# Progress-tied weight transfers, re-laid FFN buffers and epilogues in parts, in an eight-core hybrid decoder step

## The chip, the cores and the metric

The kernel runs on all 8 cores of one Trainium2 chip (two dies of four cores), one prompt sequence and 16 sample tokens per core. The metric is the device time of the slowest core, in microseconds (us). A run is called slow when some of its cores were granted a visibly lower TensorE clock and took longer; such runs are left out of all comparisons. Profiles show one execution. Where I give the idle time of TensorE by stage, I summed "idle before" over the pieces of its order of instructions; a mean is over the eight cores of one profiled execution. The stages are: start (to 125 us), middle (255 to 560 us, the passage from the mixer to the FFN), and tail (from TensorE's last instruction to the end of the span). Between 125 and 255 us and after 560 us little is idle.

## The reference, cut to what matters

```python
h = rmsnorm(x, g_pre_mix)
u, v, bg, cg, ga, gb = split(h @ w_in)                   # 1024 -> 4096
a = multiscale_pool(u, ...)                              # causal windows 2, 4, 8, 16, then w_pool
b = (bg * causal_dwconv(cg * v)) @ w_conv_out
x = x + rmsnorm((sigmoid(ga) * a + sigmoid(gb) * b) @ w_o, g_post_mix)
h = rmsnorm(x, g_pre_ffn)
gate, val = split(causal_dwconv(h @ w_up))               # 1024 -> 2 x 2816
x = x + rmsnorm((silu(gate) * val) @ w_down, g_post_ffn)
```

A core has 2080 tokens. Phase A (the mixer) takes them in five tiles of 416, phase B (the FFN) in six of 344.

## The kernel before

Every operation is put into a list with the buffers that it reads and writes. A small list scheduler then models durations and fixes the order of instructions on each engine: among the operations that are ready it takes the one that was listed first. Waits follow from the buffers' dependencies only. A tile's two epilogues, the small work after its mixing, are the residual (scale, add the reloaded x, square, store) and the normalisation (eight products and the h2T store).

One input projection block, F, has 16 groups of 8 matmuls (128); mixing, Bfull, has 8 merge steps of 21 matmuls and an output projection, WO, of 64. The order is F(0), F(1), Bfull(0), F(2), Bfull(1), F(3), Bfull(2), F(4), Bfull(3), Bfull(4), then phase B. XR is the buffer into which x is read again for the residual; H2S holds the normalised result, which the h2T store takes to memory; WO writes its squares over H2S.

```python
def F(t, hooks={}):
    for i in range(16):
        F_block(t, i, hooks)
    if t < NTA - 1:                      # the last columns become the next tile's first: the halo copies
        S.add("pool", lambda e: e.tensor_copy(out=U.ap[:, :, 1:16], in_=U.ap[:, :, NA + 1:UW]), ...)
        S.add("pool", lambda e: e.tensor_copy(out=P.ap[:, :, 2:4], in_=P.ap[:, :, NA + 2:NA + 4]), ...)
    ...
# start: weights in order, the conversion to bf16 done by POOL's transfers
for i in range(4):
    wload(W_IN, w_in, i, 1, BL)
load_x(1, 2)
for i in range(4, 16, 2):
    wload(W_IN, w_in, i, 2, BL)
...
# passage: FFN weights, as fast as their buffers come free
    if t == NTA - 1:
        for i in range(4):
            wload(W_UP, w_up, 4 * i, 4, BL)
    ...
    Bfull(t, hooks)
    if t + 2 < NTA:
        F(t + 2, {3: [lambda: epi_r(t)]})      # the whole residual epilogue in one place
for i in range(4, 11):
    wload(W_UP, w_up, 4 * i, 4, BL)
for m in range(8):
    wload(W_DN, w_dn, m, 1, FC * 128)
...
# end: residual added in memory by accumulating transfers from POOL
for q in range(4):
    dve(... Y *= rstd ...)
    pool_dma(yT[...], Y.ap[...], ..., acc=True, mx=4096)
```

Of the kernel before, what the change touches and what calls it, by code (L numbers as in the profile page):

```python
# [12 lines left out]
NS = 16  # L13
D = 1024
KC = 8
# [41 lines left out]
class Sched:  # L57
# [10 lines left out]
    def add(self, eng, fn, r=(), w=(), dma=False, dur=0.0, byts=0, pri=0, tab=None):  # L68
# [22 lines left out]
        deps = set(raw)  # L91
        for d in oth:
            dop = self.ops[d]
            if dop.eng == eng and eng == "pe":
                continue
            deps.add(d)
# [132 lines left out]
def build_nc():  # L229
# [77 lines left out]
    X = al(KC, NA)  # L307
    H = [al(KC, NA, True) for _ in range(2)]
    UW = NA + 16
    U = al(4, UW)  # L310
    PW = NA + 8
# [5 lines left out]
    MERGED = al(KC, NA, True)  # L317
# [3 lines left out]
    STG = al(1, 200)  # L321
    R = Buf(SBW - KC * NA, KC, NA, False)
# [5 lines left out]
    ST_POOL = Buf(X.off, 4, 15 * NS, False)  # L328
    ST_CONV = Buf(X.off + 960, 4, 2 * NS, False)

    bl = Alloc(W0 + 32 * 512, SBW)
    W_UP2 = bl(12, KC * 128, True)
    W_UP = Buf(W0, 44, KC * 128, True)
    W_DN = bl(8, FC * 128, True)
    H2W = NB + 8
    H2 = [bl(KC, H2W, True) for _ in range(2)]
    G = [bl(FC, NB, True)]
    NSET = 4
    TB = [bl(2, NB) for _ in range(NSET - 1)]
    TB.append(Buf(SD.off + NA, 2, NB, False))  # L340
    assert TB[-1].off + TB[-1].words <= SD.off + SD.words
    PRE = bl(44, NS)
# [6 lines left out]
    ST_FFN = Buf(H2[1].off, 44, 2 * NS, False)  # L349
    assert ST_FFN.words <= H2[1].words  # L350
    assert NTB % 2 == 0
    TAIL = Buf(H2[0].off, 1, 44 * 18, False)

# [26 lines left out]

    def pe(mms, r, w, n, start=True, stop=True):
        def f(e):
            last = len(mms) - 1
            for i, (o, l, x) in enumerate(mms):
                ins = e.matmul(o, lhsT=l, rhs=x, start=(start and i == 0), stop=(stop and i == last))  # L385
            return ins
        S.add("pe", f, r, w, dur=len(mms) * (n / 2.4 + 2.5))

    def sp_dma(out, in_, r, w, byts, pri=0):
        S.add("sp", lambda e: e.dma_start(out=out, in_=in_), r, w, dma=True, byts=byts, pri=pri)  # L390

    def pool_dma(out, in_, r, w, byts, acc=False, mx=8192, pri=0):
        if acc:
            S.add("pool", lambda e: e.dma_start(out=out, in_=in_, accum_op=ALU.add, max_dma_last_dim=mx),  # L394
                  r, w, dma=True, byts=byts, pri=pri)
        else:
            S.add("pool", lambda e: e.dma_start(out=out, in_=in_, max_dma_last_dim=mx), r, w, dma=True,  # L397
                  byts=byts, pri=pri)
# [3 lines left out]
    def wload(buf, src, lo, n, per, src_lo=None):  # L402
        src_lo = lo if src_lo is None else src_lo
        dst = buf.flat[:, lo * per:(lo + n) * per]
        pool_dma(dst, src[:, src_lo * per:(src_lo + n) * per], [], [buf.t(lo, n)], 128 * n * per * 4)
# [5 lines left out]
    def load_x(t, parts):  # L411
        st = KC // parts
        X = xbuf(t)
        for q in range(parts):
            sp_dma(X.flat[:, q * st * NA:(q + 1) * st * NA], xT[t][:, q * st * NA:(q + 1) * st * NA],
                   [], [X.t(q * st, st)], 128 * st * NA * 4)
# [120 lines left out]
    def F(t, hooks={}):  # L537
        for i in range(16):
            F_block(t, i, hooks)
        if t < NTA - 1:  # L540
            S.add("pool", lambda e: e.tensor_copy(out=U.ap[:, :, 1:16], in_=U.ap[:, :, NA + 1:UW]),
                  [U.t()], [U.t()], dur=250)
            S.add("pool", lambda e: e.tensor_copy(out=P.ap[:, :, 2:4], in_=P.ap[:, :, NA + 2:NA + 4]),  # L543
                  [P.t()], [P.t()], dur=200)
# [65 lines left out]
    def epi_r(t):  # L610
        rstd(XSQ2, 1, NA)
        tt = pool_tt if t == NTA - 1 else dve
        for q in range(2):
            sp_dma(XR.flat, xT[t][:, 4 * q * NA:4 * (q + 1) * NA], [], [XR.t()], 128 * 4 * NA * 4)
            for h in range(2):
                k, n = 4 * q + 2 * h, 2
                r = R.ap[:, k:k + n, :]
                tt(lambda e, r=r: e.tensor_tensor(out=r, in0=r, in1=SD.ap[:, 1, :].unsqueeze(1).to_broadcast([128, 2, NA]),
                                                   op=ALU.mult), [R.t(k, n), SD.t(1, 1)], [R.t(k, n)], n * NA, pri=BG)
                tt(lambda e, r=r, h=h: e.tensor_tensor(out=r, in0=r, in1=XR.ap[:, 2 * h:2 * h + 2, :], op=ALU.add),  # L620
                    [R.t(k, n), XR.t(2 * h, 2)], [R.t(k, n)], n * NA, pri=BG)
                act(lambda e, k=k, r=r: e.activation(out=XSQ2.ap[:, k:k + 2, :], in_=r, func=AF.Square),  # L622
                    [R.t(k, n)], [XSQ2.t(k, n)], n * NA, pri=BG)
            sp_dma(yT[:, 4 * q:4 * q + 4, t * NA:(t + 1) * NA], R.ap[:, 4 * q:4 * q + 4, :],
                   [R.t(4 * q, 4)], [("y", t, q)], 128 * 4 * NA * 4)

    def epi_x1(t):
        rstd(XSQ2, 2, NA)
        for k in range(KC):
            if t == NTA - 1:  # L630
                act(lambda e, k=k: e.activation(out=R.ap[:, k, :], in_=R.ap[:, k, :], func=AF.Copy, scale=cc(C_G3 + k)),
                    [R.t(k, 1), KCST, ("y", t, k // 4)], [R.t(k, 1)], NA, ap=1)
                pool_tt(lambda e, k=k: e.tensor_tensor(out=H2S.ap[:, k, :], in0=R.ap[:, k, :], in1=SD.ap[:, 2, :], op=ALU.mult),  # L633
                        [R.t(k, 1), SD.t(2, 1)], [H2S.t(k, 1)], NA)
                continue
            dve(lambda e, k=k: e.scalar_tensor_tensor(out=H2S.ap[:, k, :], in0=R.ap[:, k, :], scalar=cc(C_G3 + k),  # L636
                                                      in1=SD.ap[:, 2, :], op0=ALU.mult, op1=ALU.mult),
                [R.t(k, 1), SD.t(2, 1), KCST], [H2S.t(k, 1)], NA, stt=True, pri=BG)
        for q in range(2):
            sp_dma(h2T[:, 4 * q:4 * q + 4, t * NA:(t + 1) * NA], H2S.ap[:, 4 * q:4 * q + 4, :], [H2S.t(4 * q, 4)],  # L640
                   [("h2", t, q)], 128 * 4 * NA * 2)
# [13 lines left out]
    def pair(t, j):  # L655
# [5 lines left out]
        for half in range(2):  # L661
            b = next_bank()
            blk = 2 * j + half
            wb = W_UP.ap[:, blk, :].rearrange("p (k c) -> p k c", k=KC)
            pe([(bank(b, NBH), wb[:, k, :], hb.ap[:, k, 0:NBH]) for k in range(KC)], [W_UP.t(blk, 1), hb.t()],
# [35 lines left out]
    def epi_y(t):  # L701
        rstd(YSQ, 0, NB)
        lo = T0B + t * NB
        for q in range(4):
# [7 lines left out]
    def pre_ffn():  # L712
# [5 lines left out]
        S.add("pool", lambda e: e.tensor_tensor(out=PRE.ap, in0=st[:, :, 0, :], in1=w0b, op=ALU.mult),  # L718
              [ST_FFN.t(), KCST], [PRE.t()], dur=du)
        S.add("pool", lambda e: e.tensor_tensor(out=st[:, :, 0, :], in0=st[:, :, 1, :], in1=w1b, op=ALU.mult),  # L720
              [ST_FFN.t(), KCST, PRE.t()], [ST_FFN.t()], dur=du)
        S.add("pool", lambda e: e.tensor_tensor(out=PRE.ap, in0=PRE.ap, in1=st[:, :, 0, :], op=ALU.add),
              [ST_FFN.t(), PRE.t()], [PRE.t()], dur=du)


    load_x(0, 4)
# [6 lines left out]
    for i in range(4):  # L733
        wload(W_IN, w_in, i, 1, BL)
    load_x(1, 2)
    for i in range(4, 16, 2):
        wload(W_IN, w_in, i, 2, BL)
# [4 lines left out]
    load_x(2, 2)  # L742
    wload(W_POOL, w_pool, 0, 8, 128)
    for i in range(8):
        wload(W_IN, w_in, 16 + 2 * i, 2, BL)
        wload(W_CO, w_co, i, 1, 512)
    for i in range(4):
        wload(W_O, w_o, 2 * i, 2, BL)

    def pre_hook(t):  # L750
# [7 lines left out]
        def nh():  # L758
            prenorm_h(t)
            if t == NTA - 1:  # L760
                load_states()
            elif t > 1:
                load_x(t + 1, 2)
# [15 lines left out]
    sp_dma(o_pool_sa, st_pool_d[:, :, NS:15 * NS], [], ["o3"], 128 * 896 * 4)  # L779
    sp_dma(o_conv_st, st_conv_d, [], ["o5"], 128 * 128 * 4)  # L780
    sp_dma(o_ffn_st, st_ffn_d, [], ["o7"], 128 * 1408 * 4)
    F(1)
    for t in range(NTA):
        hooks = {}
        if t + 2 < NTA:
            sq, st, nh = pre_hook(t + 2)
            hooks = {0: [sq], 4: [st], 7: [nh]}
        if t == NTA - 1:
            hooks = {0: [lambda: epi_r(t - 1)], 5: [lambda: epi_x1(t - 1)]}
        if t == NTA - 1:  # L790
            for i in range(4):
                wload(W_UP, w_up, 4 * i, 4, BL)
        if 0 < t < NTA - 1:
            hooks.setdefault(4, []).append(lambda: epi_x1(t - 1))
        Bfull(t, hooks)
        if t + 2 < NTA:
            F(t + 2, {3: [lambda: epi_r(t)]})
    for i in range(4, 11):
        wload(W_UP, w_up, 4 * i, 4, BL)
    for m in range(8):  # L800
        wload(W_DN, w_dn, m, 1, FC * 128)
    load_h2(0)
    pre_ffn()
    WD = {2: 0, 5: 1, 8: 2, 10: 3, 13: 4, 15: 5, 18: 6, 21: 7}
    for t in range(NTB):
        for j in range(FC):
            pair(t, j)
            if t == 0 and j == 3:
                epi_r(NTA - 1)
            if t == 0 and j == 8:  # L810
                load_h2(1)
            if t == 0 and j == 17:
                epi_x1(NTA - 1)
# [143 lines left out]
```

## Time and profile before

| | before |
|---|---|
| time, median of 3 runs | 977.16 us (967.63 to 992.52, the last one slow) |
| span of core 0, the slowest | 978.1 us, of the others 962.5 to 971.5 |
| TensorE busy, core 0 / mean of 8 cores | 854 / 840 us |
| TensorE idle, start / 125 to 255 / middle / after 560 us, mean | 43.1 / 6.2 / 58.0 / 3.9 us |
| tail, mean | 18.1 us |

How to read it: TensorE has 1920 matmuls of 416 columns and 3216 of 344 or 346, at full clock 810 us (the working is in the prediction). What exceeds 810 us of busy time is low clock; cores 0 and 1 had more of it in this execution (granted 0.930, busy 854 and 857 us) than the other six (0.949 to 0.953, 835 us on the mean). The rest of the span is idle time, and each hole has to be read from what ended it.

### The profile page before, as it was taken

What the parts mean: (1) busy time and instruction counts of PE and PEld (TensorE: products, weight loads), DVE (VectorE), ACT (ScalarE), POOL (GpSimd) and SP (SyncE); (2) the same over time, 40 slices, a digit from 0 to 9 for tenths busy, and PEclk for the clock granted to TensorE, in tenths of its full rate; (3) what the DMA queues carried; (4) which work ended last, traced back from release to release, by engine and by line L of the source; (5) the groups of instructions that cost most, each with busy time, mean ns of one, the idle gap of its engine ahead of it and who ended that gap; (6) DMA issues with size and microseconds to landing.
All of it is one profiled execution on the core that took longest, in us unless ns stands there. A gap on an engine that the chain in (4) does not pass through costs nothing.

```text
span 978.1 us, 16306 instructions; the slowest of 8 cores (962.5 to 978.1 us)
## 1 busy us (share of the span) xinstructions
PE 854.3 (87%) x5136; PEld 512.0 (52%) x5136; DVE 536.2 (55%) x959; ACT 457.0 (47%) x880; POOL 221.9 (23%) x288
## 2 busy tenths in 40 slices
PE   1964999899899399964879999999999999999992
PEld 0432555455455144422546666666666666666661
DVE  1533647657667352640457656665666665675611
ACT  3212254545554044431667555654655564555531
POOL 2111000000002000030286322422432332253322
PEclk9977999999999778866789999999999999999996
DMA  9999130340327945889522000500400130040044
GB/s 201 174 186 166 24 105 24 83 140 22 100 79 114 194 127 94 168 191 174 92 71 70 32 1 2 88 1 2 74 16 1 40 49 1 2 59 1 2 75 58
DMA packets 37667, 75.82 MB, mean 78 GB/s; under 512 B 2096, under 2 KB 26544, under 8 KB 37568
## 3 DMA queue, kind: packets, MB, share of 16 engines
q0 software_dynamic: 16160, 37.56, 25.8%
q1 hardware_dynamic: 21424, 37.23, 12.5%
q8 instruction: 43, 0.70, 0.3%
q14 instruction: 40, 0.33, 0.1%
HBM read 82.14 MB, written 22.98 MB: 107 GB/s over the span
## 4 chain that ended last, share of the span: by engine, by line
PE 66%; DMA 16%; DVE 6%; issue 4%; ACT 3%; POOL 2%; POOLq 0%; DVEq 0%; SPq 0%; ACTq 0%
PE ps L385 66%; DMA big<-w_in 8%; DMA big<-xT 5%; DMA h2T<-big 3%; DVE big L673 1%; DVE big L476 1%; DVE big L620 1%; ACT L423 1%; ACT big L669 1%; DVE big L452 1%; POOL big L633 1%; DVE big L583 0%; DVE big L581 0%; DVE big L636 0%; POOL big L677 0%
## 5 line engine op out<-in xcount | busy, mean ns | idle before, releaser
L385 PE MATMUL ps<-big 128*128 128x346 bf16 (+2 forms) x5136 | 854.3, 331 | 105.9 <-ACT big L595 15.3
L385 PEld LDWEIGHTS ps<-big 128*128 128x128 bf16 x5136 | 512.0, 100 | 447.8 <-issue 136.4
L673 DVE SCALAR_TENSOR_TENSOR big<-ps,big 128x344 f32<-128x344 f32 x528 | 282.8, 572 | 186.7 <-ACT big L669 154.5
L686 POOL TENSOR_TENSOR big<-big 128x344 bf16<-128x344 f32 x132 | 120.5, 915 | 263.5 <-DVE big L673 219.5
L669 ACT ACTIVATE big<-ps,big 128x344 f32<-128x344 f32 x264 | 140.6, 545 | 72.9 <-PE ps L385 69.1
L685 ACT ACTIVATE big<-big 128x344 f32<-128x344 f32 x132 | 64.3, 488 | 39.5 <-DVE big L673 36.9
L566 ACT ACTIVATE big<-ps 128x416 f32<-128x416 f32 x80 | 39.6, 517 | 66.9 <-PE ps L385 64.7
L577 DVE SCALAR_TENSOR_TENSOR big<-ps,big 128x416 f32<-128x416 f32 x40 | 26.0, 649 | 51.1 <-PE ps L385 48.0
L696 ACT ACTIVATE big<-ps,big 128x344 f32<-128x344 f32 x48 | 26.0, 547 | 56.8 <-PE ps L385 50.5
L593 ACT ACTIVATE big<-ps,big 128x416 f32<-128x416 f32 x40 | 24.6, 620 | 38.7 <-PE ps L385 38.6
L705 DVE TENSOR_TENSOR big<-big 128x688 f32<-128x688 f32 x24 | 19.4, 870 | 36.3 <-ACT big L425 36.3
L394 POOL DMA_DIRECT2D yT<-big x24 | 29.5, 1880 | 36.8 <-DVE big L705 36.8
L521 DVE TENSOR_TENSOR big<-ps,big 128x416 f32<-128x416 f32 x20 | 11.6, 586 | 47.0 <-ACT big L519 25.2
L622 ACT ACTIVATE big<-big 128x832 bf16<-128x832 f32 x20 | 17.8, 892 | 41.2 <-DVE big L620 40.7
L397 POOL DMA_DIRECT2D big<-w_up x11 | 7.8, 712 | 123.6 <-PE ps L385 123.6
L452 DVE SCALAR_TENSOR_TENSOR big<-big 128x416 f32<-128x416 f32 x40 | 25.9, 650 | 14.0 <-ACT big L449 11.9
L595 ACT ACTIVATE big<-ps 128x416 bf16<-128x416 f32 x40 | 20.1, 530 | 28.9 <-DMA h2T<-big 28.9
L476 DVE TENSOR_TENSOR big<-big 128x430 f32<-128x430 f32 (+3 forms) x50 | 30.0, 601 | 2.7
L543 POOL COPY big<-big 128x8 f32<-128x8 f32 x4 | 1.4, 346 | 131.6 <-DVE big L452 131.6
L435 DVE SCALAR_TENSOR_TENSOR big<-big 128x416 bf16<-128x416 f32 x40 | 23.0, 646 | 12.4 <-ACT big L425 10.8
L620 DVE TENSOR_TENSOR big<-big 128x832 f32<-128x832 f32 x16 | 16.0, 1020 | 25.0 <-DMA big<-xT 25.0
L429 ACT ACTIVATE big<-big 128x832 bf16<-128x832 f32 x20 | 17.1, 887 | 25.9 <-DMA big<-xT 25.9
(49 smaller groups left out, 312.4 us busy)
## 6 DMA issues: line engine op xcount, KB each, us to landing
big<-xT SPq DMA_DIRECT2D x18, 832.0 KB, 7.0
big<-w_up POOLq DMA_DIRECT2D x11, 1024.0 KB, 14.3
yT<-big SPq DMA_DIRECT2D x10, 832.0 KB, 5.3
yT<-big POOLq DMA_DIRECT2D x24, 344.0 KB, 8.3
big<-w_in POOLq DMA_DIRECT2D x14, 512.0 KB, 28.1
big<-w_dn POOLq DMA_DIRECT2D x8, 704.0 KB, 16.9
h2T<-big SPq DMA_DIRECT2D x10, 416.0 KB, 4.0
big<-h2T SPq DMA_DIRECT2D x6, 692.0 KB, 4.9
```

Source lines behind the costliest of these rows:

```text
L385: ins = e.matmul(o, lhsT=l, rhs=x, start=(start and i == 0), stop=(stop and i == last))
L394: S.add("pool", lambda e: e.dma_start(out=out, in_=in_, accum_op=ALU.add, max_dma_last_dim=mx), r, w, dma=True, byts=byts, pri=pri)
L452: dve(lambda e, k=k: e.scalar_tensor_tensor(out=cv, in0=p[:, 2 + k:2 + k + NA], scalar=cc(C_WC + 4 * k + c), in1=cv, op0=ALU.mult, op1=ALU ...
L476: dve(lambda e, nx=nx, cur=cur, s=s, lo2=lo2: e.tensor_tensor(out=nx.ap[:, 0, lo2:UW], in0=cur[:, lo2:UW], in1=cur[:, lo2 - s:UW - s], op= ...
L566: act(lambda e, b=b, g=g: e.activation(out=GT.ap[:, g, :], in_=bank(b, N), func=AF.Sigmoid), [("ps", b)], [GT.t(g, 1)], N, psum=True, tab= ...
L577: dve(lambda e: e.scalar_tensor_tensor(out=A_, in0=bank(bp, N), scalar=cc(C_PS + m), in1=A_, op0=ALU.mult, op1=ALU.mult), [("ps", bp), GT. ...
L620: tt(lambda e, r=r, h=h: e.tensor_tensor(out=r, in0=r, in1=XR.ap[:, 2 * h:2 * h + 2, :], op=ALU.add), [R.t(k, n), XR.t(2 * h, 2)], [R.t(k, ...
L669: act(lambda e, b=b, fj=fj, tt=tt: e.activation(out=tt, in_=bank(b, NB), func=AF.Copy, scale=cc(C_WF + fj)), [("ps", b), KCST], [tok], NB, ...
L673: dve(lambda e, b=b, fj=fj, tt=tt, k=k: e.scalar_tensor_tensor(out=tt, in0=ps[:, b * 512 + k:b * 512 + k + NB], scalar=cc(C_WF + 44 * k + ...
L685: act(lambda e: e.activation(out=g, in_=g, func=AF.Silu), [T.t(0, 1)], [T.t(0, 1)], NB, tab="silu")
L686: S.add("pool", lambda e: e.tensor_tensor(out=gb.ap[:, j, :], in0=g, in1=v, op=ALU.mult), [T.t()], [gb.t(j, 1)], dur=NB * 2.17 + 100)
L696: act(lambda e: e.activation(out=Y.ap[:, m, :], in_=bank(b, NB), func=AF.Copy, scale=cc(C_G4 + m)), [("ps", b), KCST], [Y.t(m, 1)], NB, ps ...
```

## The change

Its intent: let the FFN weights arrive during the last mixing stages, at TensorE's pace rather than in a burst, by laying them over mixer buffers that are dead by then; keep the epilogues from blocking an engine for long; order the first transfers; shorten the end. The core of the diff, with cuts marked:

```diff
-    def add(self, eng, fn, r=(), w=(), ..., tab=None):
+    def add(self, eng, fn, r=(), w=(), ..., tab=None, after=()):
+        deps.update(x.idx for x in after if x is not None)
 ...
+    W_UP = Blocks([W0 + BW * i for i in range(16)] + [U.off + BW * i for i in range(13)] +
+                  [W0 + BW * (16 + i) for i in range(15)])
+    W_DN = Buf(W0 + 31 * BW, 8, FC * 128, True)
 ...
-    def pool_dma(out, in_, r, w, byts, acc=False, mx=8192, pri=0):
+    def pool_dma(out, in_, r, w, byts, acc=False, mx=4096, pri=0, after=()):
 ...
+    def wup(n):          # the next n blocks of W_UP, tied to TensorE's latest listed matmul
+            pool_dma(dst.flat, w_up[:, i * BL:k * BL], [], [dst.t()], ..., after=[last_pe[0]])
 ...
-            S.add("pool", lambda e: e.tensor_copy(out=U.ap[:, :, 1:16], ...
+            act(lambda e: e.activation(out=U.ap[:, :, 1:16], in_=U.ap[:, :, NA + 1:UW], func=AF.Copy), ...
 ...
+    wd = [wload(W_IN, w_in, i, 1, BL, after=[x0[1]]) for i in range(16)]
+    load_x(1, 2, after=[wd[5]])
 ...
     wload(W_POOL, w_pool, 0, 8, 128)
+    for i in range(16):
+        w = wload(W_IN, w_in, 16 + i, 1, BL)
+        if i % 2:
+            wload(W_CO, w_co, i // 2, 1, 512)
 ...
+            for i in range(4):
+                hooks[i] += er[1 + i:2 + i]          # residual epilogue, a quarter per merge step
+            o = 1 if t == NTA - 1 else 0
+            hooks[4 + o] += ex[0:2]                  # normalisation, in three more steps
+            hooks[5 + o] += ex[2:5]
+            hooks[6 + o] += ex[5:9]
 ...
+        if t >= NTA - 2:
+            for m in range(8):
+                if t == NTA - 2 or m % 2:
+                    hooks[m].append(lambda: wup(2))
 ...
+                add = pool_tt if q < 2 else dve      # last tile: residual added on chip
+                add(lambda e, yq=yq, q=q: e.tensor_tensor(out=yq, in0=yq, in1=X1.ap[...], op=ALU.add), ...)
+                sp_dma(yT[:, 2 * q:2 * q + 2, lo:lo + NB], yq, ...)
```

The epilogues' background priority in the scheduler (`pri=BG`) went with the split. Three copies of states inside memory moved to phase B.

## The prediction

> **What bounds the kernel now.** I read the page first, then the windows of busy time, the order of instructions on TensorE, and the chain of work that ended last. All lines are of core 0, the slowest (978.1 us; the other cores 962.5 to 971.5). The page's row of 40 slices (24.5 us each), cut to TensorE, its clock and the DMA engines:
>
> ```profile
> PE   1964999899899399964879999999999999999992
> PEclk9977999999999778866789999999999999999996
> DMA  9999130340327945889522000500400130040044
> ```
>
> TensorE is the bound nearly everywhere, with three holes: the first four slices, the stretch from the 13th to the 21st, and the last slice. Both inner holes lie under a DMA row near 9, and the clock is low in the same places. The windows give sizes (columns: stretch, length, busy us and count for PE, PEld, DVE, ACT, POOL, then clock, DMA share, GB/s):
>
> ```profile
> 206.00:300.00 94.00, 89.44 (x506) 49.32 (x507) 60.04 (x104) 48.94 (x86) 1.92 (x3) 1.00 0.25 76
> 344.00:402.00 58.00, 57.31 (x261) 28.27 (x262) 25.12 (x42) 25.88 (x45) 2.31 (x4) 0.79 0.55 112
> 402.00:440.00 38.00, 28.90 (x127) 13.57 (x125) 19.78 (x31) 11.15 (x17) 8.54 (x9) 0.73 0.89 194
> 440.00:470.00 30.00, 14.70 (x63) 7.21 (x62) 0.00 (x0) 5.06 (x11) 2.15 (x3) 0.67 1.04 173
> 700.00:850.00 150.00, 150.00 (x1026) 100.27 (x1025) 97.45 (x179) 81.87 (x164) 49.14 (x51) 1.00 0.15 25
> ```
>
> A 416-column matmul takes 89.44/506 = 177 ns at full clock, but 57.31/261 = 220 ns from 344 to 402 us, at clock 0.79; a 344-column one takes 146 ns. The floor follows: the kernel has 1920 matmuls of 416 columns (phase A, the mixer, five token tiles) and 3216 of 344 or 346 (phase B, the FFN, six tiles): 1920 x 0.177 + 3216 x 0.146 = 340 + 470 = 810 us. The page has 854 us busy, so a low clock costs 44 us, and 978 - 854 = 124 us are idle.
>
> Where the idle time lies, from TensorE's order of instructions (start, length, then the idle time before and its releaser):
>
> ```profile
> 23.81 23.14 PE L385 MATMUL ps<-big 128*128 128x416 bf16 x120 [7.32 <-DVE big L435]
> 54.05 4.97 PE L385 MATMUL ps<-big 128*128 128x416 bf16 x16 [7.10 <-DMA big<-w_in]
> 61.82 11.54 PE L385 MATMUL ps<-big 128*128 128x416 bf16 x56 [2.80 <-DVE big L435]
> 86.33 3.97 PE L385 MATMUL ps<-big 128*128 128x416 bf16 x11 [12.97 <-ACT big L519]
> ```
>
> 43 us are lost before 86.3 us. The last hole, 13 us, is not a missing weight. ScalarE waits to write the conv buffer until POOL has copied its halo, and POOL is held in its instruction order by weight-transfer issues:
>
> ```profile
> 84.17 1.15 POOL L397 DMA_DIRECT2D big<-w_o  x2 [1.56 <-DMA big<-w_in]
> 85.32 0.20 POOL L543 COPY big<-big 128x8 f32<-128x8 f32 x1
> ...
> 85.67 0.93 ACT L519 ACTIVATE big<-ps 128x416 f32<-128x416 f32 x2 [25.64 <-POOL big L543]
> ```
>
> The second hole: the FFN weights begin at 296 us and are issued as fast as buffers come free, and small transfers that the epilogues need sit among them. The three longest such pieces of the chain of work:
>
> ```profile
> 314.36 27.03 DMA big<-xT
> ...
> 405.27 17.58 DMA big<-xT
> ...
> 439.86 29.34 DMA h2T<-big
> ```
>
> The 832 KB reload of x usually lands in 7 us (median); here it took 27. The h2T store frees the buffer that the last output projection writes, so TensorE stood still for 12 us. From 300 to 540 us the windows sum to 49 us idle. The tail is 18 us: TensorE ends at 960.1, VectorE scales until 964.7, and four accumulating transfers from POOL land by 978:
>
> ```profile
> 961.47 3.23 DVE L705 TENSOR_TENSOR big<-big 128x688 f32<-128x688 f32 x4 [19.54 <-ACT big L425]
> 962.90 4.89 POOL L394 DMA_DIRECT2D yT<-big  x4 [17.75 <-DVE big L705]
> ```
>
> 43 + 49 + 18 leaves 14 us scattered elsewhere.
>
> **What the skill says.** "DMA: Bandwidth & Descriptors", section "Issuing engines are not separate DMA queues": transfers started by different engines share the same 16 DMA engines. The 7 us that became 27 agrees. "HBM Reference", section "Specifications (TRN2)": about 358 GB/s per core when both of a pair stream. Here the first 98 us moved x tiles 5.1 MB, mixer weights 23.6 MB as float32, state copies 1.25 MB and constants 0.1 MB: 30.1/98 = 307 GB/s, somewhat lower; I use 307. "TensorE: Matmul & The Clock Gate", "Back-to-back issue gap": columns/2.4 + 2.5 ns when warm, so 176 and 146 ns: agrees. The same page, Part 1, says that an idle array drops to half clock and that three busy cores of a die pull it to 13/16. The 0.81 does appear, but 700 to 850 us run at 1.00 with all eight cores busy, so the trace does not agree that it lasts; here low clock follows the holes.
>
> **The change part by part.**
>
> Start. The first weight transfer now waits for the second quarter of x, x1 and x2 come after chosen weights, and the 1.25 MB of state copies move to phase B. Estimated from 307 GB/s: half of x lands at 5 us, normalising it takes what it took (12 us from first square, 6.3, to first product, 18.97, minus the 7 us it waited for late quarters and constants, then 4.6 us of products), so TensorE starts near 17 us instead of 23.8. The sixteen W_IN blocks of 0.52 MB and x1 (1.7 MB) need 33 us after 8 us: block 15 lands near 41 us, and F(0) ends at 42.5. After that DMA runs ahead: a merge step eats 1.3 MB (4.3 us of DMA) per 29 matmuls (5.1 us). The halo copies go to ScalarE at about 0.2 us each, so the 13 us hole goes. Idle to the end of tile 0 falls from 47 us (43 plus 3.5 between 86 and 150) to about 20: -27. The low clock there (72 matmuls at 229 ns in 50:84 and 50 at 233 ns in 86:98) is worth another 4 to 6.
>
> Middle. Of 23 MB of W_UP, 10 blocks go during F(4), 16 during mixing of tile 3, 8 during tile 4, and 10 in phase B, each pair of blocks issued only when TensorE has passed a point. This is possible since the new blocks lie over W_IN blocks and mixer buffers dead after F(4). Estimate of the load: 17.8 MB plus 10 MB of epilogue traffic in 95 us of TensorE work is 27.8/0.307 = 91 us. It fits, barely, but no backlog stands in front of a small transfer. W_DN, 11.5 MB = 38 us, flows during phase B tile 0 and is used 15 us or more after. The epilogues are cut into one part per merge step, and 8.2 us of them (8 x 1.02) leave F, where VectorE was full (18 + 8 us against 22.5 us), for the merge stretch (33 of 41 us). Tile 4 reads X in place rather than reloading. I expect 8 of the 49 us idle to stay: -41. Without long holes the clock should stay up: of core 0's 34 us excess in 300:540 (596 matmuls at about 220 instead of 177 ns = 25, and 369 at 169 instead of 146 = 8.5) perhaps half returns, -17. Cores 2 to 7 had only some 15 us of it, so there less.
>
> Tail. The last tile adds x1 on chip: after the scale factor 4 multiplies and 2 adds on VectorE, 6 x 0.87 = 5.2 us, POOL's two adds of 1.8 us beside them, then a plain store of about 3 us (344 KB; 416 KB halves took 4.0 us): 961.5 + 8.2 = 969.7 against 978.1: -8.
>
> Against it: phase B tile 0 has VectorE at 4 x 0.572 = 2.29 us per pair against TensorE 16 x 0.146 = 2.34, so any ScalarE delay shows; more, smaller DMA issues on POOL (about 30 more at 0.55 us, beside other work); rounding and stalls. +5.
>
> Sum: 978 - 27 - 5 - 41 - 17 - 8 + 5 = 885 on core 0; from the faster cores' clock (busy 831 to 838) with 50 us idle comes 970 - 27 - 5 - 41 - 5 - 8 + 5 = 889. From the floor: 810 + 20 + 8 + 10 scattered + 10 tail + 15 to 20 low clock = 873 to 878. The two ways differ by what clock I grant; I take 880.
>
> **Rivals.** First, DMA becomes the bound from F(4) to phase B tile 0: W_UP and W_DN with the epilogue traffic are near 95% of 307 GB/s. For it: 91 of 95 us. Against: the first use of a late block is 40 us after its issue, and accumulated slack absorbs some. If it fails, h2T stores again hold the output projection, some 15 to 25 us: 895 to 905. Second, the limiter: a denser kernel on eight cores may be held at 13/16 for long. For it: cores 0 and 1 stayed at 0.81 through 57 us of dense matmuls. Against: 400 us of phase B at 1.00. If all phase A ran at 220 ns it would cost 1920 x 43 ns = 82 us: 950 or so. Third, the start transfer is hidden anyway: if only the order of holes changes because W_IN bandwidth paces F(0) and then mixing, the start yields 15, not 32: 895.
>
> **Range and chances.** All three losses known by size point to TensorE going from 87% to about 94% busy. A gain under 2% needs most of 93 us to return as new waits, so faster 0.97, within 2% 0.02, slower 0.01. Range 858 to 905, its upper end the first or third rival, its lower end a nearly full clock.
>
> **What would show it.** Right: first dense matmuls near 17 us, no idle over 3 us between 43 and 110 us, no ScalarE wait for a POOL halo copy; x reloads and h2T stores under 12 us; TensorE idle from F(4) to phase B under 15 us; last store under 11 us after TensorE ends; TensorE idle about 50 us in all. Wrong: DMA rows of 9 together with TensorE waits on ScalarE's output-projection copies, or on W_UP or W_DN; a clock near 0.81 over more than 150 us; POOL waits that hold products in phase B tiles 0 and 1.

## The result, and the profile after

The changed kernel took 888.83 us, median of 4 runs (883.52 to 903.11; the run of 903.11 was slow); the kernel before 972.59 us, median of 4. The ratio of the fast runs is 0.9137, 95% interval 0.9062 to 0.9212: faster. A ratio here is the mean time of one kernel's fast runs over that of the other's of the same rounds, so it is not quite the ratio of the medians. Later, beside other kernels on another chip, the same kernel measured 0.9144 (0.9122 to 0.9167).

| TensorE | before, core 0 | after, core 0 | before, mean | after, mean |
|---|---|---|---|---|
| span | 978.1 | 886.1 | 969.6 | 880.4 |
| busy | 854.4 | 821.8 | 840.3 | 820.8 |
| idle, start | 43.3 | 28.8 | 43.1 | 26.6 |
| idle, 125 to 255 us | 6.6 | 0 | 6.2 | 0 |
| idle, middle | 52.0 | 19.9 | 58.0 | 17.3 |
| idle, after 560 us | 3.9 | 3.1 | 3.9 | 3.1 |
| tail | 18.0 | 12.5 | 18.1 | 12.6 |

The rows of 40 slices (now 22.2 us each), cut as in the prediction:

```profile
PE   1789999999999787889999999999999999999994
PEclk9999999999999988989999999999999999999997
DMA  9999421250227992646994014003201400030061
```

One of the two inner holes is gone, the other is shallow, and the clock row is nearly all 9. The DMA row is spread out: the FFN weights now fill slices 13 to 21. The order of TensorE's instructions, core 0 (start, length, idle before, releaser):

```profile
23.48 13.02 PE L406 MATMUL ps<-big 128*128 128x416 bf16 x64 [6.39 <-DMA big<-w_in]
...
41.77 1.57 PE L406 MATMUL ps<-big 128*128 128x416 bf16 x8 [3.39 <-DMA big<-w_in]
...
57.35 53.61 PE L406 MATMUL ps<-big 128*128 128x416 bf16 x304 [0.99 <-DVE big L469]
...
313.60 10.15 PE L406 MATMUL ps<-big 128*128 128x416 bf16 x49 [8.22 <-ACT big L658]
...
339.53 27.71 PE L406 MATMUL ps<-big 128*128 128x416 bf16 x145 [4.80 <-ACT big L627]
```

The 13 us hole before 86 us is gone: after 57 us TensorE runs for 53 us in one piece. But the dense part starts at 23.5 us, hardly sooner than before. Two waits are left in the middle, and the chain of work that ended last shows what they stand on:

```profile
294.81 16.54 DMA big<-xT
...
322.90 15.88 DMA h2T<-big
```

The x reload of the residual and the h2T store are shorter than the 27 and 29 us of before, but still three to four times their medians (5.2 and 4.1 us). For the reload the comparison flatters: it now moves 416 KB at a time, before 832 KB. The start, all engines' order, POOL's lines (the number after x counts transfers):

```profile
1.68 0.75 POOL L418 DMA_DIRECT2D big<-w_pool  x1 [0.28 <-issue]
2.41 1.11 POOL L418 DMA_DIRECT2D big<-w_in  x2
...
3.49 0.56 POOL L418 DMA_DIRECT2D big<-w_co  x1
4.01 0.57 POOL L418 DMA_DIRECT2D big<-w_in  x1
...
7.16 1.60 POOL L418 DMA_DIRECT2D big<-w_in  x3 [2.58 <-DMA big<-xT]
```

Five transfers leave before x has landed. They are W_POOL, later W_IN blocks and W_CO, which have no `after`: they were listed later, but they were ready, so the scheduler took them while W_IN block 0 was still waiting for x. And the tail:

```profile
874.94 3.89 DVE L749 TENSOR_TENSOR big<-big 128x688 f32<-128x688 f32 x3 [19.54 <-ACT big L459]
876.03 4.29 POOL L752 TENSOR_TENSOR big<-big 128x688 f32<-128x688 f32 x2 [17.54 <-DVE big L749]
...
879.00 2.05 DVE L752 TENSOR_TENSOR big<-big 128x688 f32<-128x688 f32 x1 [0.17 <-DVE big L749]
```

A product or an add of 688 elements takes VectorE 0.87 us alone. Here three take 3.89 and one takes 2.05 while POOL adds.

### The profile page after: what moved, and what is told of

Same layout as the page of the kernel before. It is cut to its first block, busy times and chain, and to the rows that moved or that the text cites. A ratio compares the mean times of both kernels' runs of the same rounds, so it can differ in the third digit from the quotient of the medians.

```text
span 886.1 us, 16478 instructions; the slowest of 8 cores (877.3 to 886.1 us)
## 1 busy us (share of the span) xinstructions
PE 821.7 (93%) x5136; PEld 503.3 (57%) x5136; DVE 540.8 (61%) x961; ACT 456.7 (52%) x888; POOL 234.9 (27%) x308
## 3 DMA queue, kind: packets, MB, share of 16 engines
q0 software_dynamic: 22720, 36.15, 27.5%
## 4 chain that ended last, share of the span: by engine, by line
PE 78%; DMA 9%; DVE 6%; ACT 2%; issue 2%; POOL 1%; DVEq 0%; SPq 0%; ACTq 0%; POOLq 0%
PE ps L406 78%; DMA big<-xT 4%; DMA big<-w_in 3%; DMA h2T<-big 2%; DVE big L714 1%; DVE big L510 1%; ACT big L710 1%; DVE big L749 1%; DVE big L675 1%; DVE big L469 0%; DVE big L656 0%; POOL big L727 0%; DVE big L517 0%; DVE big L752 0%; DVE big L613 0%
## 5 line engine op out<-in xcount | busy, mean ns | idle before, releaser
L406 PE MATMUL ps<-big 128*128 128x416 bf16 (+2 forms) x5136 | 821.7, 323 | 51.9 <-ACT big L463 15.0
L406 PEld LDWEIGHTS ps<-big 128*128 128x128 bf16 x5136 | 503.3, 98 | 370.0 <-issue 71.9
L418 POOL DMA_DIRECT2D big<-w_up x23 | 16.1, 699 | 284.1 <-PE ps L406 274.0
L486 DVE SCALAR_TENSOR_TENSOR big<-big 128x416 f32<-128x416 f32 x40 | 25.9, 651 | 22.5 <-ACT big L483 20.4
L658 ACT ACTIVATE big<-big 128x832 bf16<-128x832 f32 x20 | 17.9, 897 | 30.0 <-DVE big L656 29.5
L510 DVE TENSOR_TENSOR big<-big 128x430 f32<-128x430 f32 (+3 forms) x50 | 30.1, 601 | 4.6 <-ACT big L560 1.5
L415 POOL DMA_DIRECT2D yT<-big x20 | 24.5, 1862 | 18.2 <-DVE big L757 18.2
L555 DVE TENSOR_TENSOR big<-ps,big 128x416 f32<-128x416 f32 x20 | 11.7, 588 | 26.5 <-PE ps L406 26.1
L418 POOL DMA_DIRECT2D big<-w_in x32 | 17.0, 534 | 39.8 <-DMA big<-w_in 31.7
L739 ACT ACTIVATE big<-ps 128x344 bf16<-128x344 f32 x48 | 21.6, 450 | 10.5 <-PE ps L406 10.5
L483 ACT ACTIVATE big<-big 128x416 f32<-128x416 f32 x20 | 12.7, 639 | 27.8 <-DVE big L555 27.8
L757 DVE TENSOR_TENSOR big<-big 128x688 f32<-128x688 f32 x20 | 16.2, 870 | 16.7 <-ACT big L459 16.7
```

The source lines that it names most:

```text
L406: ins = e.matmul(o, lhsT=l, rhs=x, start=(start and i == 0), stop=(stop and i == last))
L418: return S.add("pool", lambda e: e.dma_start(out=out, in_=in_, max_dma_last_dim=mx), r, w, dma=True, byts=byts, pri=pri, after=after)
L486: dve(lambda e, k=k: e.scalar_tensor_tensor(out=cv, in0=p[:, 2 + k:2 + k + NA], scalar=cc(C_WC + 4 * k + c), in1=cv, op0=ALU.mult, op1=ALU ...
L510: dve(lambda e, nx=nx, cur=cur, s=s, lo2=lo2: e.tensor_tensor(out=nx.ap[:, 0, lo2:UW], in0=cur[:, lo2:UW], in1=cur[:, lo2 - s:UW - s], op= ...
```

## The experiments

Twelve experiments ran, all with correct results. The times in brackets are medians of fast runs. Numbers 1, 3, 8 and 9 ran on a chip where most runs were slow (granted clock near 0.95 on pairs of cores), so that each has one fast run only.

**1. Halo copies back on POOL, in the changed kernel.**

```diff
-            act(lambda e: e.activation(out=U.ap[:, :, 1:16], in_=U.ap[:, :, NA + 1:UW], func=AF.Copy), ...
+            S.add("pool", lambda e: e.tensor_copy(out=U.ap[:, :, 1:16], in_=U.ap[:, :, NA + 1:UW]), ...   # P likewise
```

> The changed kernel with the two halo copies put back on POOL. Theory (the 13 us hole of the kernel before was POOL's instruction order, a copy queued behind weight-transfer issues): the hole comes back in the second input projection, TensorE idle before 110 us rises from 28 us by 8 to 15 us, the time by 8 to 15 us over the changed kernel (about 897 to 903). Rival (the copies find a free place now that the transfers are single blocks, and the ScalarE move is worth nothing): within 3 us of the changed kernel (888).

Idle at the start rose from 26.6 to 46.8 us, idle elsewhere by about 1 us, busy time by 2.4 us, and the fast run took 911.4 us. TensorE's order on the slowest core, and POOL's at the end of the hole:

```profile
55.20 10.01 PE L406 MATMUL ps<-big 128*128 128x416 bf16 x56 [0.75 <-DVE big L469]
90.03 40.31 PE L406 MATMUL ps<-big 128*128 128x416 bf16 x217 [24.82 <-ACT big L553]
```

```profile
88.04 0.53 POOL L418 DMA_DIRECT2D big<-w_o  x1 [2.18 <-DMA big<-w_co]
88.56 0.24 POOL L575 COPY big<-big 128x60 f32<-128x60 f32 x1
```

TensorE filled the seven PSUM banks (its output memory) with 56 matmuls and then stood for 24.8 us. In POOL's order the copies came at 88.6 us, after the last W_O issue at 88.0. The theory holds; the size is larger than expected, because this start reaches the second projection sooner and so waits longer for the same end of the transfers.

**2. The same two copies on ScalarE, in the kernel before, as the only change.**

> The kernel before with one part of the change alone: the two halo copies on ScalarE. Putting them back on POOL in the changed kernel brought 20 us of idle back at the start. Theory (this copy alone is the hole before 86 us): idle before 125 us falls from 43 us to 26 to 30, the time by 13 to 17 us (fast runs about 957). Rival (in the kernel before, the later mixer weights come too late and TensorE waits for them in place of the copy): under 5 us.

Idle at the start fell from 43.1 to 28.8 us, the other idle times stayed within about 4 us, ratio to the kernel before 0.9835 (0.9806 to 0.9864) (954.9 us); the interval lies clear of 1. One line's move from one engine to another is worth 16 of the change's 84 us (1 - 0.9835 = 1.65% of some 970 us, against 972.6 - 888.8).

**3. Weights not tied to TensorE.** Everything else of the change stays; the transfers keep their buffers' dependencies.

```diff
-            pool_dma(dst.flat, w_up[:, i * BL:k * BL], [], [dst.t()], 128 * (k - i) * BL * 4, after=[last_pe[0]])
+            pool_dma(dst.flat, w_up[:, i * BL:k * BL], [], [dst.t()], 128 * (k - i) * BL * 4)
-            wload(W_DN, w_dn, dn[0], 1, FC * 128, after=[last_pe[0]])
+            wload(W_DN, w_dn, dn[0], 1, FC * 128)
```

> The changed kernel with FFN weight transfers no longer waiting for TensorE's progress; layout, places in program order and split epilogues stay. Theory (pacing keeps the transfers that the epilogues need short): from 270 to 390 us the x reloads and h2T stores take 20 us or more again, TensorE idle there rises from 20 us to 35 to 50, and the time to about 905 to 915. Rival (the gain of the middle comes from the new layout and the split alone; the buffers' own dependencies pace the transfers): within 4 us of the changed kernel, idle there about 20.

Idle in the middle rose from 17.3 to 23.8 us, the mean span from 880.4 to 889.1 us (893.3 us, one fast run). Both expectations missed, the rival narrowly: the tie is worth something, but not the main part.

**4. Epilogues undivided, weights tied; and 5. undivided and untied.** Both keep the new layout, the early place of the weights, the start and the tail. The epilogues go back to one block each at their old places in program order, the residual one inside F, so size and place change together. The next tile's square and statistics also go back to merge steps 0 and 4. The old background priority was not restored.

```diff
-            for i in range(4):
-                hooks[i] += er[1 + i:2 + i]
-            ...
+            if t == NTA - 1:
+                hooks[0] += er[1:5]
+            hooks[5 if t == NTA - 1 else 4] += ex
-            fh = {12: er[0:1]}
+            fh = {3: er}
```

> The changed kernel with the epilogues put back as undivided blocks at the places where the kernel before had them (first part after block 3 of the input projection, second in merge step 4 or 5); weights stay paced, the layout stays. Theory (the split is a main part of the middle's gain): idle from 125 to 560 us rises from 17 to 25 us or more and the time by 8 us or more. Rival (pacing and layout alone do it): within 3 us.

> The changed kernel with both undone: undivided epilogues and weights not tied to TensorE, so the new layout, the earlier place of the weights, the start and the tail are what is left. Theory A (layout and the earlier weights bring most of the middle): idle from 255 to 560 us between 22 and 32 us against a mean of 58 before. Theory B (without pacing and split the layout brings nothing): 45 us or more.

| mean of 8 cores | span | busy | idle 125 to 255 | idle middle | fast runs |
|---|---|---|---|---|---|
| split, tied (the change) | 880.4 | 820.8 | 0 | 17.3 | 887.9 |
| split, untied | 889.1 | 823.9 | 0 | 23.8 | 893.3 |
| undivided, tied | 913.3 | 831.9 | 11.7 | 27.2 | 920.6 |
| undivided, untied | 909.6 | 830.0 | 11.6 | 25.6 | 915.4 |
| kernel before | 969.6 | 840.3 | 6.2 | 58.0 | 970 to 976 |

Undividing costs 33 us of mean span: 11.7 + 9.9 us of idle and 11 us of low clock. The kernel before had 6.2 us idle from 125 to 255 us, so part of the 11.7 may be the missing priority; that was not tried. TensorE's order on the slowest core of the fourth kernel:

```profile
322.52 28.53 PE L406 MATMUL ps<-big 128*128 128x416 bf16 x148 [11.51 <-DVE big L566]
```

L566 is the last VectorE product of an input projection: with the whole residual epilogue inside F, VectorE is late for it. In F(2) it came 3.0 us late without a wait on a transfer, close to the prediction's count (18 + 8 us of work in 22.5 us). In F(4), shown here, one step further back stands the x reload again:

```profile
312.20 1.03 DVE L656 TENSOR_TENSOR big<-big 128x832 f32<-128x832 f32 x1 [5.75 <-DMA big<-xT]
```

Of the 12.0 us that TensorE stood here (mean of eight cores), VectorE had itself waited 5.1 us for the reload, with the projection's products behind it in its order. With undivided epilogues the tie to TensorE brings nothing (913 against 910). Even so, undivided and untied, the middle has 25.6 us idle against 58.0 before, so theory A of the fifth run stands: the new layout with the early weights brought the larger part of the middle's idle time, together with what this run also kept (x reloads in halves, tile 4's x used in place, smaller transfer pieces). I did not try the layout quite alone.

**6. Thinner weights in tile 3's mixing, thicker in tile 4's.**

```diff
-                if t == NTA - 2 or m % 2:
+                if t == NTA - 1 or m > 3:
```

> The changed kernel with the FFN weights spread more thinly where they met the epilogue: during mixing of tile 3 they start only with merge step 4 (8 blocks instead of 16), during tile 4 they go at every step (16 instead of 8). Theory (in mixing of tile 3, 1.05 MB per merge step of 21 matmuls, 3.7 us, is 284 of 307 GB/s, so that a 416 KB x reload took 16.5 us and an h2T store 15.9 us): the x reload in merge steps 0 to 3 lands in under 8 us, the 8 us wait of TensorE near 305 us goes, idle from 255 to 560 us falls from a mean of 17 us to 6 to 10, the time by 7 to 11 us (fast runs about 877 to 880). Rival (the same bytes only collide later, in tile 4's mixing and before phase B's first products): idle there stays 14 us or more, the time within 3 us.

The rival came true: idle in the middle 17.8 us (17.3), ratio 0.9148 (888.0 us). The reload in tile 3's mixing no longer held TensorE, but the one in tile 4's mixing did. The chain on the slowest core has the same two pieces, with the long x reload later:

```profile
312.46 17.40 DMA h2T<-big
...
351.51 16.53 DMA big<-xT
```

**7. Less in both mixing stretches, more in phase B.** Eight blocks move from tile 3's mixing to phase B tile 0.

```diff
-                if t == NTA - 2 or m % 2:
+                if m % 2:
-                if j >= 10 and j % 2 == 0:
+                if j >= 14 and j % 2 == 0:        # W_DN, in phase B tile 0
```

> The changed kernel with eight FFN weight blocks moved out of the mixing of tile 3 altogether: 8 blocks there and 8 in tile 4's mixing (every second merge step), 18 instead of 10 in phase B tile 0; W_DN begins two pairs later twice over. Theory (moving the load to tile 4 in the run before only moved the collision, so the sum in both mixing stretches has to fall): x reloads and h2T stores from 285 to 390 us land in under 10 us, TensorE idle from 255 to 560 us falls from 17 us to 6 to 10, the time by 7 to 10 us (fast runs about 878). Rival (phase B tile 0 then waits for weights: 18 blocks are 9.4 MB, 31 us of its 51): TensorE waits on W_UP or W_DN appear after 390 us and the time is not better.

Idle in the middle fell to a mean of 14.1 us only (884.7 us, ratio 0.9106, interval 0.9082 to 0.9130, against 0.9144 for the changed kernel on that chip: the intervals touch). The first half of the theory holds in direction only: on the slowest core the reload took 10.9 us and the h2T store 12.2 us, not under 10. And the rival holds in part: there TensorE waited 6.9 us for a W_UP block at 446 us.

```profile
294.69 10.92 DMA big<-xT
...
317.47 12.24 DMA h2T<-big
```

```profile
446.35 331.50 PE L406 MATMUL ps<-big 128*128 128x346 bf16 x2246 [6.91 <-DMA big<-w_up]
```

**8. Later mixer weights held behind x too.** W_POOL, W_IN 16 to 31, W_CO and W_O get the same `after=[x0[1]]` as the first sixteen blocks.

```diff
-    wload(W_POOL, w_pool, 0, 8, 128)
+    wload(W_POOL, w_pool, 0, 8, 128, after=[x0[1]])
-        w = wload(W_IN, w_in, 16 + i, 1, BL)
+        w = wload(W_IN, w_in, 16 + i, 1, BL, after=[x0[1]])     # W_CO, W_O likewise
```

> The changed kernel with the later mixer weights (W_POOL, W_IN 16 to 31, W_CO, W_O) made to wait for the second quarter of x too. In the changed kernel five of them, about 2.4 MB read, were issued at 1.7 to 4.6 us ahead of W_IN block 0, which no one had meant. Theory (they delay x and the first weights): W_IN block 0 becomes the first transfer, dense matmuls start near 18 us instead of 23.5, the first projection ends 5 to 7 us sooner, the time falls by 5 to 7 us (about 882). Rival (first projection is paced by the sum of bytes, or lost again behind x1): under 2 us.

TensorE's order, core 0:

```profile
18.25 16.28 PE L406 MATMUL ps<-big 128*128 128x416 bf16 x80 [6.30 <-DVE big L469]
...
51.71 56.00 PE L406 MATMUL ps<-big 128*128 128x416 bf16 x304 [4.66 <-DVE big L469]
```

The dense part starts at 18.3 to 19.4 us on all cores, 5 us sooner on core 0 and 4 on the mean. Idle at the start fell by 3.4 us only (26.6 to 23.2), since the second projection now waits 4.7 us for the normalisation of x1 (881.8 us, one fast run). So the five early transfers did delay the start, and part of that was lost again behind x1; the gain lies between the theory's 5 to 7 us and the rival's 2.

**9. The accumulating end restored in the changed kernel.** The on-chip add of the last tile and its loads are taken out.

> The changed kernel with the last tile's on-chip add undone: four accumulating transfers from POOL as in the kernel before. Theory: the time from TensorE's last matmul to the end goes from 12.5 us back to 18 us, the whole by 5 to 6 us (about 894). Rival (the plain store and the two adds cost as much as the accumulation): within 2 us.

The tail became 16.1 us instead of 12.6 (889.2 us, one fast run): the on-chip add is worth 3.5 us. The kernel before has 18.1 us. The other 2 us lie in the landing of the last transfers: VectorE's four products (3.23 us) and POOL's four issues (4.9 us) take the same in both, but from POOL's last issue to the end pass 10.3 us on core 0 before and 7.9 here (core 3: 10.4 and 8.9). Why they land sooner is open.

**10. All mends together.** The thin weights, the held mixer weights, x1 after W_IN block 3 instead of 5, the FFN-state products listed in phase B, and in the tail all adds on VectorE (`add = dve`).

> The thin weights, the held later mixer weights, x1 two weight blocks earlier, the POOL products of the FFN state moved from the last merge steps to phase B's start (where VectorE reads one operand from PSUM), and all last adds on VectorE, together. Expected: idle before 125 us 20 us (27 in the changed kernel, 23 with the held weights alone), idle from 255 to 560 us 5 to 8 us, tail 11.5 us (12.6: POOL's adds held two VectorE products for 1.2 to 1.4 us beyond their 0.87), the time about 866 in fast runs, 2.4% under the changed kernel. Rival (the gains overlap, or the denser kernel is granted a lower clock): above 878.

878.0 us, not the 866 expected; ratio 0.9049 (0.9032 to 0.9067). The tail is 11.5 us as expected: eight VectorE instructions of 0.87 us with no POOL beside them beat six of which two were stretched. Start 22.3 us. But the middle is 13.1 us, not 5 to 8: on the slowest core TensorE waited 1.9 and 7.3 us for W_UP blocks in phase B tile 0. And moving POOL's products in the list had moved nothing: they were ready early, and the scheduler put them where they had been.

**11. The changed kernel again**, on the same chip as 7 and 10.

> The changed kernel itself, unaltered, beside the two above on the same chip: fast runs between 882 and 890, idle before 125 us about 27 us, from 255 to 560 us about 17 us, tail 12.6 us, as in its first profile. If it differs by more than 1%, the comparisons across chips above are not to be trusted to that degree.

886.8 us, ratio 0.9144; start 25.7, middle 16.3, tail 12.6 us. It repeats within 1%.

**12. Spread evenly, and with a real tie for POOL's products.** On top of 10:

```diff
-                for i in range(7, 16, 2):         # W_UP in F(4): from its middle
+                for i in range(1, 12, 2):         # from its start
-                if j % 2 == 0:                    # phase B tile 0: at every second pair
-                    wup(2)
-                if j >= 14 and j % 2 == 0:
+                wup(2)                            # at every pair
+                if j >= 10 and j % 2 == 0:
-              [ST_FFN.t(), KCST], [ST_FFN.t()], dur=du)
+              [ST_FFN.t(), KCST], [ST_FFN.t()], dur=du, after=[last_pe[0]])
```

> The run before (all mends together) left two waits in the middle: TensorE on W_UP blocks in phase B tile 0 (up to 1.9 + 7.3 us on core 4), since 18 blocks there were issued one pair of blocks per two products; and 2.2 us ahead of the last output projection, because the instruction scheduler had put POOL's two FFN-state products where they always were, although their place in the program was later. Here the transfers in phase B go at every product pair, 12 blocks go in F(4) from its start instead of 10 from its middle, and the POOL products wait for the last output projection. Theory: both waits go, the three VectorE products beside POOL take 1.95 us instead of 4.4, idle from 255 to 560 us falls from a mean of 13 us to 4 to 7, the time by 6 to 8 us (fast runs about 871). Rival (the bytes of one stretch are only pushed into the next again, x reloads in tile 3's mixing or the x tile 4 epilogue): idle there stays above 10 us and the time above 875.

It took 867.6 us; ratio 0.8906 (0.8846 to 0.8965), the best of all and under both kernels. (The record marks this run's class as unclear, not as faster; two of its six executions and five of the eleven of the kernel before were slow. Its fast runs, 865.5 to 868.4, lie under every other fast run here.) Idle in the middle fell to a mean of 4.9 us, busy to 817.0 us. The page's rows of the profiled core:

```profile
PE   2888999999999989999999999999999999999994
PEclk9999999999999999999999999999999999999998
```

The VectorE products that stood beside POOL's, in the changed kernel (first line, core 0) and in this one (second, core 3):

```profile
380.69 4.48 DVE L675 SCALAR_TENSOR_TENSOR big<-big 128x416 bf16<-128x416 f32 x3
```

```profile
361.53 1.77 DVE L675 SCALAR_TENSOR_TENSOR big<-big 128x416 bf16<-128x416 f32 x3
```

The Trainium skill, "SBUF — State Buffer", section "Who interferes with whom", says that a VectorE instruction with two SBUF inputs contends with a GpSimd (POOL) instruction that reads SBUF. The runs agree: 0.87 us became up to 2.31 and 0.65 up to 2.22 beside POOL, and went back without it.

## Why the prediction was right, and where it was off

The class and the size were right: 880 predicted, 888.83 measured, in the range. That on core 0 the sum of 885 met a span of 886.1 is luck: three terms fell short, the clock gave more than was granted, and the stalls did not come.

**Floor and idle plus clock as the account.** Right. 92.0 us of span on core 0 are 59.4 of idle time and 32.6 of busy time, and every piece has a place in the table.

**Start, -27 us.** Measured -18 on core 0 (46.8 to 28.8 us). The halo copy was right, and the largest single line that was tried alone: run 2. The failed step is "TensorE starts near 17 us instead of 23.8" (the terms shown, 5 + 12 - 7 + 4.6, make some 15; the rest is not told). It rested on "the first weight transfer now waits for the second quarter of x", which is true for sixteen transfers only. Five without a tie went first. Run 8 gave the 18 us, and showed a second limit that I had not seen, x1's normalisation: 23.2 us of idle stayed, not 20.

**Middle, -41 us, 8 us to stay.** Measured -32 on core 0, 17.3 us left on the mean. The failed step is the load: "It fits, barely, but no backlog stands in front of a small transfer", from 27.8 MB over 95 us. The average over 95 us was not the rate that mattered. A merge step has 21 matmuls, 3.7 us; the rest of the 232 are the output projection. So W_UP was asked for at 1.05 MB / 3.7 us = 284 of 307 GB/s through all of tile 3's mixing, with the reload in the same microseconds. From 300 to 320 us on core 0 the DMA engines were 0.93 to 1.05 busy and TensorE worked 11.8 of the 20 us. That is the first rival in part: it cost at most some 12 us (17.3 to 4.9 in run 12, which also moved POOL's products, worth about 2), not 15 to 25. I also gave the middle to layout and pacing and priced the split at nothing of its own. Runs 3 to 5 show that with the split in place the tie brings 6.5 us of idle, and that the split, with its place outside F, brings up to 22 us of idle time and 11 us of clock (the old priority was not restored).

**Clock, -5 and -17 us on core 0.** Measured -32.6; against the floor of 810 us the low clock costs 12 us instead of the 15 to 20 that I granted. Much of core 0's share belongs to that one execution of the kernel before: from 345 to 402 us, with TensorE 99% busy, cores 0 and 1 were granted 0.79 and 0.80, cores 2 to 4 0.95 to 0.99. On cores 2 to 7 busy time fell from 835.2 to 820.8 us, 14 us against the 10 of the second sum. Low clock and holes mostly went together: 11 us more of it with the undivided epilogues, 817 us busy with the fewest holes; but run 1, with 20 us more idle, had only 2.4 us more. So the prediction's "low clock follows the holes" is an inference, and does not explain cores 0 and 1. The second rival, 13/16 held for long, did not show in the fast runs: from 390 to 860 us core 0 did 3176 matmuls in 467.2 us, 147 ns each.

**Tail, -8 us.** Measured -5.5. The failed step is "POOL's two adds of 1.8 us beside them". They were not free: they took 2.1 and 2.3 us, and VectorE's six instructions took 7.9 us from first to last, not 5.2 (run 10: all eight on VectorE, 11.5 us tail).

**Stalls, +5 us.** Not seen: 3.1 us of idle after 560 us against 3.9 before, and none from 387 to 777 us.

**The third rival**, a start paced by the weights that yields 15 us and not 32, came true in part: on core 0 the start yielded 18 us of idle and, as an estimate, 6 of clock (122 matmuls from 50 to 98 us at 229 and 233 ns before; 176 ns from 47 to 110 us after).

Of the signs, these held: no ScalarE wait on a POOL halo copy, and no idle over 3 us between 43 and 110 us (longest 1.6 on core 0). Missed were 17 us for the first dense matmuls, transfers under 12 us, idle under 15 us from F(4) to phase B, the last store within 11 us, and 50 us of idle in all (64 on core 0). One sign of being wrong did show: TensorE stood 4.8 us for ScalarE's output-projection copy (L627) while the DMA engines were 0.90 busy (330 to 340 us).

Left open: the smaller transfer pieces (`mx` 4096, 22,720 packets instead of 16,160 on the software queue) were not tried alone, nor were the reloads in halves, the layout, or the old priority with undivided epilogues; and why the transfers of run 9 land 2 us sooner.

## What to carry to other kernels

A tie on some transfers is not an order: whatever is ready and has no tie goes ahead of them, so look in the trace for what was issued first, and hold the rest too. Size paced transfers by the bytes per step over the duration of that very step, beside everything else that moves in it, and then look where the collision went; it tends to move rather than go. A small copy on an engine that also issues bulk transfers can cost more than all of the arithmetic that one is tempted to tune.

## What the Trainium skill lacked or had wrong

- "TensorE: Matmul & The Clock Gate", Part 1, has three or more busy cores of a die held at 13/16 of the clock while the load lasts. Here all eight ran dense matmuls from 390 to 860 us at a granted clock of 1.00 (147 ns for 344 to 346 columns). It does show in some of the slow runs, left out above: the four cores of one die had a mean of 0.813 to 0.818 in a run of 1025.5 us (experiment 10) and 0.797 to 0.800 in one of 1103.4 us (the kernel before); in most slow runs it was pairs of cores near 0.95.
- "DMA: Bandwidth & Descriptors", "Issuing engines are not separate DMA queues", says that transfers share the engines, but gives no figure for a small transfer under bulk load: a 416 KB x reload took up to 16.5 us and a 416 KB h2T store 15.9 us, against medians of 5.2 and 4.1 us in the same execution.
- "HBM Reference" gives about 358 GB/s per core with a pair streaming; loads that convert float32 to bf16, with plain loads beside them, moved 307 GB/s (an estimate: the program's 30.1 MB, read side, over the first 98 us of the kernel before, DMA engines 1.00 busy).
- "SBUF — State Buffer", "Who interferes with whom", is right on the contention but says nothing of its size for this mix: VectorE tensor_tensor of 688 float32 elements 0.87 us alone, 2.05 to 2.31 us beside a POOL add.
